# Another order of the filler matmuls of an attention stage, and its small constants loaded earlier

## The chip, the cores and the metric

The program runs on one core of a Trainium2 chip. The metric is the device time of one execution in microseconds (us). Three timed runs of the kernel before gave 2757.0, 2759.0 and 2761.09 us (median 2759.0); the profiled execution took 2755.99 us, with a span of 2753.8 us from the first to the last instruction.

## The reference

Two layers act on 1024 latent tokens and 256 context tokens of width 1024. Each layer normalises and modulates its input and multiplies it by one wide matrix; the columns of the product feed four branches, whose outputs are gated, projected, merged and added back.

```
z    = split_cols(h @ w_in)              # pool_in 256, mla_*, diff_*, swa_*, gates 1024, merge 4096
pool = windowed means (2, 4, 8, 16 tokens) of pool_in, minus pool_in, times w_pool, times s_pool
mla  = dense softmax attention over 1280 keys, 4 heads (latent branch)
diff = two dense softmax maps per head, map 1 - lam * map 2, 4 heads; normalised
       lam = exp(sum(lam_q1*lam_k1)) - exp(sum(lam_q2*lam_k2)) + lam_init
swa  = windowed attention, 128-token blocks, 256 context keys + up to 3 blocks, with a sink logit
x    = x + gate * rms_norm(sum_r sigmoid(merge_r) * ((y_r * silu(gates_r)) @ w_br[r]) @ w_out)
```

In layer 0 the 256 context tokens are queries too; in layer 1 only the 1024 latent tokens are.

## The kernel before, in words

Everything is fp32. A dense product is done as three matmuls per 128 rows of the contraction: a number is split into a rounded high part and the rest, and high*high, high*low and low*high are added (`mm3`, lines 75 to 78). TensorE (PE) does the matmuls, VectorE (DVE) maxima, differences and sums, ScalarE (ACT) exponentials, copies and the rounding, GpSimd (POOL) some elementwise work and the low parts of weights. Nearly all transfers are issued by one queue, SyncE's (SP). The instructions are emitted in the order in which the Python code runs; the framework then orders each engine's instructions by that order and by when it thinks their inputs ready, and puts in the semaphores. So code order sets the order on an engine, but an instruction that is ready earlier can be moved ahead.

A layer goes through these stages:

- the latent projections and their row statistics (`st.body` in `layer`);
- the dense part: a list of column tiles of `w_in`, built by `values`, `roped`, `keys_swa`, `gates` and `pooled`. Each tile is 128 columns times 8 contraction steps times 2 or 3 chunks of tokens (512, 512 and, where the context counts, 256). A step of 512 tokens is three matmuls and counts as 3 * 0.216 = 0.648 us in the planner's money. Tiles up to the queries of the differential branch (`dense.until(W_DQ + 1)`) are run at once, together with `up_all`, which makes the latent branch's keys, values and queries;
- the attention units: for each of the 4 heads of the differential branch, 4 of the latent branch and 2 key heads of the local (windowed) branch, one unit for each block of queries: 20, 20 and 20 units in layer 0, 16, 16 and 16 in layer 1. A unit has "mains" (scores of 128 queries, line 1116, 1075 to 1077 or 1174, and their softmax in `softmax`, line 977) and turns of `pv_steps` (transposes of the probabilities, line 1005, and their products with the values, line 1021), which run one to two units behind;
- merge of the branches, `w_out`, and the next layer's normalisation.

The dense tiles that are left when the units begin are filler. After each main and each turn the loop calls `dense.fill(f)`, which emits dense steps until their planned cost reaches f; f is `FILL[l][branch]` shared over the unit's mains and turns, so a unit with all its turns gets about `FILL[l][branch]` us of filler (keys 1, 2, 3: latent, differential, local branch). `FILL[l]["pre"]` is emitted ahead of the first unit. When the list is empty, nothing is filled. The keys of the local branch must be stored before its first unit is prefetched, so `prefetch` forces the list up to `W_SQ + 1` there.

`pooled` is two tiles of the matrix and, after each, `rest`, which forms the windowed sums of a chunk on DVE (6 operations per chunk in the first, 8 in the second), multiplies them by `w_pool` with three matmuls (tiles `pd<-sh,wph` and so on), and stores the result. It counts as 0.7 us per 512 tokens in the planner. Its input lies in a buffer (`zt1`) of which there is one, shared with `values` and `roped`.

Ahead of the first unit `prefetch(0)` issues the loads of the first keys (`kt`), values (`vt`) and queries (`qt`); then `const_loads` issues four loads of the lambda rows, one of the sinks and one of the mask of the local branch (`smask`); then the filler "pre", and then `const_values`, which computes lambda. The lambda rows lie in two of the five buffers `P` of the probabilities. The weights of each filler tile are loaded (`wraw`) by the same queue, rounded by ACT (`wh`), and their rests taken by POOL (`wl`).

Of the kernel before, what the change touches and what calls it, by code (L numbers as in the profile page):

```python
# [8 lines left out]
F = mybir.dt.float32  # L9
# [10 lines left out]
T = SEQ + CTX  # L20
# [12 lines left out]
def kernel(ctx: ExitStack, tc: tile.TileContext, A: dict, out: bass.AP):  # L33
# [467 lines left out]
    def layer(l, es_prev):  # L501
# [15 lines left out]
        def lat_tile(i, dt):  # L517
            return (p1 if i > 2 else p1b).tile([128, T], dt, name=f"n{i}", tag=f"n{i}")
# [247 lines left out]
        for j in range(7):  # L766
            gates(j)
        values(W_SV, svd, 0)
        keys_swa()
        roped(W_SQ, sqd, qch, 64 ** -0.5, 4, 32, ("C64", "S64"))  # L770
        pooled()
# [16 lines left out]

        gkv = gcol("g_ckv", 0, 128)
# [99 lines left out]
        def up_all():  # L889
            nonlocal kvh, kvl, q0h, q1h, q0l, q1l  # L890
            for us in key_rope():
                yield us
            kvh, kvl, q0h, q0l = (lat_tile(i, R) for i in (0, 3, 1, 4))
# [56 lines left out]
        ls = c1.tile([128, 2], F, name="ls")  # L950
        nlam = c1.tile([128, 1], F, name="nlam")
        sink = c1.tile([128, 4], F, name="sink")
        nsink = c1.tile([128, 4], F, name="nsink")
        lam = kp.tile([128, T], F, name="P", tag="P", bufs=5)[:, 0:128].rearrange("p (a c) -> p a c", a=4)
        lt = kp.tile([128, T], F, name="P", tag="P", bufs=5)[:, 0:64].rearrange("p (a c) -> p a c", a=2)

        def const_loads():
            for i, n in enumerate(("lam_q1", "lam_k1", "lam_q2", "lam_k2")):
                dma(lam[:, i], A[n][l:l + 1, :].broadcast_to([128, 32]))
            dma(sink, A["sink"][l:l + 1, :].broadcast_to([128, 4]))  # L960
            dma(smask, A["smask"])

        def const_values():
            lv = lam.rearrange("p (a b) c -> p a b c", b=2)
            tt(lt, lv[:, :, 0], lv[:, :, 1], ALU.mult)
            nc.vector.tensor_reduce(out=ls, in_=lt, axis=AX.X, op=ALU.add)
            act(ls, ls, AF.Exp)
            tt(nlam, ls[:, 1:2], ls[:, 0:1], ALU.subtract)
            ts(nlam, nlam, -lam_init, op0=ALU.add)
            ts(nsink, sink, -1.0)  # L970
# [249 lines left out]
        const_loads()  # L1220
# [3 lines left out]
        for i, (key, keys, load, run) in enumerate(units):  # L1224
# [3 lines left out]
            for a, main in enumerate(mains):  # L1228
                main()
                if a == 0:  # L1230
                    prefetch(i + 1)
                dense.fill(f)
# [284 lines left out]
        for q, (ci, d) in enumerate(steps):  # L1517
# [30 lines left out]
    FILL = ({1: 4.1, 2: 4.9, 3: 0.8, "n": 1.5, "uk": 1.2, "uq": 1.5, "uv": 2.0, "pre": 10.0},  # L1548
            {1: 4.3, 2: 4.9, 3: 0.8, "n": 2.5, "uk": 1.2, "uq": 1.5, "uv": 2.0, "pre": 8.0})
# [114 lines left out]
```

## Time and profile before

| what | value |
|---|---|
| median of 3 runs (lowest to highest) | 2759.0 us (2757.0 to 2761.09) |
| profiled execution, its time and its span | 2755.99 us, 2753.8 us |
| PE busy | 2618.1 us, 95% |
| DVE, ACT, POOL busy | 1517.9, 1184.7, 803.6 us |
| mean granted TensorE clock, share of full | 0.978 |
| moved by DMA | 322.27 MB, mean 117 GB/s |
| layer 0: differential, latent, local units begin (first score) | 248.6, 489.2, 709.7 us |
| layer 1: differential, latent, local units begin (first score) | 1699.6, 1911.7, 2121.2 us |

Busy time is the union of an engine's instructions. Matmuls are pipelined and their ends are modelled, so PE can be shown as busy and still not be at its peak; where two stretches do like work, their lengths say more than their busy time. "Idle before, releaser" is the time that an engine stood still ahead of an instruction and what the profile believes ended it.

### The profile page before, as it was taken

What the parts mean: (1) busy time and instruction counts of PE and PEld (TensorE: products, weight loads), DVE (VectorE), ACT (ScalarE), POOL (GpSimd) and SP (SyncE); (2) the same over time, 40 slices, a digit from 0 to 9 for tenths busy, and PEclk for the clock granted to TensorE, in tenths of its full rate; (3) what the DMA queues carried; (4) which work ended last, traced back from release to release, by engine and by line L of the source; (5) the groups of instructions that cost most, each with busy time, mean ns of one, the idle gap of its engine ahead of it and who ended that gap; (6) DMA issues with size and microseconds to landing.
All of it is one profiled execution on the core that took longest, in us unless ns stands there. A gap on an engine that the chain in (4) does not pass through costs nothing.

```text
span 2753.8 us, 38441 instructions
## 1 busy us (share of the span) xinstructions
PE 2618.1 (95%) x14194; PEld 2202.6 (80%) x14194; DVE 1517.9 (55%) x2638; ACT 1184.7 (43%) x2178; POOL 803.6 (29%) x492
## 2 busy tenths in 40 slices
PE   7998999999989989999999997999999999999998
PEld 5776888888878878888877776888877788888878
DVE  7545888766754893322148554888666732233133
ACT  4433777655662211222245343777555722222231
POOL 4223343110001223333324313443110022444324
PEclk9998999999999999999999998999999999999999
DMA  6366333532334552221135266333433243222123
GB/s 237 100 199 199 117 98 91 147 121 92 98 114 136 193 171 74 76 73 62 35 106 198 81 202 207 123 106 108 136 99 97 78 129 102 79 87 86 48 77 100
DMA packets 209069, 322.27 MB, mean 117 GB/s; under 512 B 26740, under 2 KB 123634, under 8 KB 208882
## 3 DMA queue, kind: packets, MB, share of 16 engines
q1 hardware_dynamic: 208882, 319.83, 37.1%
q8 instruction: 111, 1.82, 0.3%
q14 instruction: 76, 0.62, 0.1%
HBM read 239.07 MB, written 77.86 MB: 115 GB/s over the span
## 4 chain that ended last, share of the span: by engine, by line
PE 60%; DVE 10%; issue 4%; DMA 3%; ACT 3%; POOL 1%; SPq 0%; POOLq 0%; DVEq 0%; ACTq 0%
PE pd L76 12%; PE pd L77 12%; PE pd L78 11%; PE acc L1021 5%; PE pt L1005 4%; PE pt L76 2%; PE pt L77 2%; PE pt L78 2%; DVE mjunk L150 2%; PE pss L1116 1%; PE pss L1075 1%; PE pss L1077 1%; PE pss L1076 1%; PE pd L1532 1%; DVE t L53 1%
## 5 line engine op out<-in xcount | busy, mean ns | idle before, releaser
L76 PE MATMUL pd<-h,wh 128*128 128x512 f32 (+2 forms) x2288 | 859.0, 376 | 20.8 <-ACT zt L50 9.4
L77 PE MATMUL pd<-h,wh 128*128 128x512 f32 (+2 forms) x2288 | 846.0, 370 | 0.3 <-DVE h L56 0.3
L78 PE MATMUL pd<-h,wl 128*128 128x512 f32 (+2 forms) x2288 | 846.3, 370 | 0.0
L53 POOL TENSOR_TENSOR wl<-wraw,wh 128x1024 fp32r<-128x1024 f32 x106 | 260.5, 2457 | 995.6 <-ACT wh L50 929.3
L76 PEld LDWEIGHTS pd<-h,wh 128*128 128x128 f32 (+1 forms) x2288 | 437.1, 191 | 84.9 <-ACT zt L50 10.0
L78 PEld LDWEIGHTS pd<-h,wl 128*128 128x128 f32 (+1 forms) x2288 | 435.8, 190 | 67.3 <-issue 1.5
L77 PEld LDWEIGHTS pd<-h,wh 128*128 128x128 f32 (+1 forms) x2288 | 437.3, 191 | 59.2 <-DVE h L56 1.0
L977 DVE CUSTOM_DVE_ANT_0 P<-pss,zero 128x1280 f32<-128x1280 f32 (+1 forms) x216 | 295.9, 1370 | 98.3 <-PE pss L1116 45.7
L53 DVE TENSOR_TENSOR tl<-pt,th 128x512 fp32r<-128x512 f32 (+1 forms) x420 | 276.2, 671 | 132.5 <-ACT th L50 128.9
L50 ACT ACTIVATE th<-pt 128x512 fp32r<-128x512 f32 (+1 forms) x420 | 239.5, 582 | 159.1 <-PE pt L1005 153.7
L53 DVE TENSOR_TENSOR sg<-sg,pt 128x512 f32<-128x512 f32 x96 | 65.4, 686 | 394.8 <-PE pt L78 394.8
L1005 PE MATMUL pt<-kc,P 128*128 128x128 f32 x1632 | 255.8, 276 | 4.9 <-DVE P L56 1.2
L1021 PE MATMUL acc<-th,vt 128*128 128x256 f32 x816 | 244.8, 312 | 3.4 <-ACT ot L50 1.5
L1021 PE MATMUL acc<-tl,vt 128*128 128x256 f32 x816 | 221.6, 292 | 10.0 <-DVE tl L53 9.3
L50 ACT ACTIVATE wh<-wraw 128x1024 fp32r<-128x1024 f32 x124 | 130.7, 1054 | 214.4 <-PE pd L77 162.3
L50 ACT ACTIVATE P<-P,m 128x1280 f32<-128x1280 f32 (+1 forms) x144 | 182.8, 1269 | 76.7 <-DVE m L977 75.9
L50 ACT ACTIVATE sg<-pd 128x512 f32<-128x512 f32 x128 | 75.6, 591 | 316.2 <-PE pd L78 313.3
L1005 PEld LDWEIGHTS pt<-kc,P 128*128 128x128 f32 x1632 | 191.5, 141 | 20.4 <-DVE tl L53 6.1
L53 POOL TENSOR_TENSOR m<-m,sg 128x512 f32<-128x512 f32 x96 | 131.5, 1375 | 193.7 <-DVE sg L53 192.4
L1021 PEld LDWEIGHTS acc<-th,vt 128*128 128x128 f32 x816 | 155.5, 191 | 37.4 <-ACT th L50 20.5
L1021 PEld LDWEIGHTS acc<-tl,vt 128*128 128x128 f32 x816 | 155.7, 191 | 30.3 <-DVE tl L53 21.3
L50 ACT ACTIVATE P<-P,negm 128x1280 f32<-128x1280 f32 (+3 forms) x144 | 146.5, 1017 | 75.8 <-DVE negm L977 75.3
(291 smaller groups left out, 3917.8 us busy)
## 6 DMA issues: line engine op xcount, KB each, us to landing
wraw<-in_w_in_dram SPq DMA_DIRECT2D x108, 512.0 KB, 3.5
wmt<-in_w_modt_dram SPq DMA_DIRECT2D x64, 256.0 KB, 3.1
wraw<-in_w_out_dram SPq DMA_DIRECT2D x32, 512.0 KB, 3.3
yd<-ot SPq DMA_DIRECT2D x108, 128.0 KB, 1.8
kt<-dkd SPq DMA_DIRECT2D x64, 160.0 KB, 3.1
qt<-dqd SPq DMA_DIRECT2D x72, 128.0 KB, 2.8
ya<-yd SPq DMA_DIRECT2D x36, 256.0 KB, 3.0
yb<-yd SPq DMA_DIRECT2D x36, 256.0 KB, 3.0
```

Source lines behind the costliest of these rows:

```text
L50: return nc.scalar.activation(out=o, in_=i, func=func, **kw)
L53: return (e or nc.vector).tensor_tensor(out=o, in0=a, in1=b, op=op)
L76: nc.tensor.matmul(ps, wh(k), xh(k), start=k == 0, stop=False)
L77: nc.tensor.matmul(ps, wh(k), xl(k), start=False, stop=False)
L78: nc.tensor.matmul(ps, wl(k), xh(k), start=False, stop=k == n - 1)
L150: nc.vector.tensor_tensor_reduce(out=jk, in0=a, in1=b, scale=1.0, scalar=start, op0=ALU.mult, op1=ALU.add, accum_out=o)
L977: nc.vector.tensor_tensor_reduce(out=o, in0=i, in1=zero.to_broadcast([128, nk]) if mask is None else mask, scale=-1.0, scalar=1e30 if h is ...
L1005: t = nc.tensor.transpose(pt[:, 2 * j + i, :], Ps[i][:, (g + j) * 128:(g + j + 1) * 128], ident)
L1021: nc.tensor.matmul(acc, vt[:, kts[g + j], :], x[:, j, :], start=g + j == 0 and a == 0, stop=g + j == nk - 1 and a == 1)
L1075: nc.tensor.matmul(o, qt[0:96, 0, qs], kh[0:96, ks], start=True, stop=False)
L1076: nc.tensor.matmul(o, qt[0:96, 0, qs], kl[0:96, ks], start=False, stop=False)
L1077: nc.tensor.matmul(o, qt[0:96, 1, qs], kh[0:96, ks], start=False, stop=True)
```

## The change

- The tiles of the dense part get another order. Before: gates 0 to 6, values, keys and queries of the local branch, pooling, gate 7. After: gates 0 to 5, pooling, values, keys and queries of the local branch, gates 6 and 7.
- `FILL` is changed: local branch 0.8 to 1.4 in layer 0, 0.8 to 1.3 in layer 1; in layer 1 also the latent branch 4.3 to 3.7 and the differential branch 4.9 to 4.6.
- The four lambda rows and the sinks are loaded when the dense part is set up, into tiles of their own, and the two sums of lambda are taken in `up_all`; only the exponential and the last steps stay in `const_values`.
- The mask of the local branch is loaded at the third differential unit, once the fourth unit's inputs are requested.

```diff
--- before.py
+++ after.py
@@ -763,12 +763,13 @@
         values(W_DV + 1, dvd, 2)
         roped(W_DK, dkd, ALL, 1.0, 8, 16, ("C32", "S32"))
         roped(W_DQ, dqd.rearrange("m a d n -> a m d n"), qch, 32 ** -0.5, 8, 16, ("C32", "S32"))
-        for j in range(7):
+        for j in range(6):
             gates(j)
+        pooled()
         values(W_SV, svd, 0)
         keys_swa()
         roped(W_SQ, sqd, qch, 64 ** -0.5, 4, 32, ("C64", "S64"))
-        pooled()
+        gates(6)
         gates(7)
 
         p1b = pool(f"mlb{l}", 1, es_m)
@@ -786,6 +787,11 @@
             split(raw, h, lo)
             return h, lo
 
+        ls, nlam, sink, nsink = (sta.tile([128, w], F, name=n) for n, w in (("ls", 2), ("nlam", 1), ("sink", 4), ("nsink", 4)))
+        lam = p1.tile([128, 4, 32], F, name="lam")
+        for i, n in enumerate(("lam_q1", "lam_k1", "lam_q2", "lam_k2")):
+            dma(lam[:, i], A[n][l:l + 1, :].broadcast_to([128, 32]))
+        dma(sink, A["sink"][l:l + 1, :].broadcast_to([128, 4]))
         gkv = gcol("g_ckv", 0, 128)
         gq0 = gcol("g_cq", 0, 128)
         gq1 = gcol("g_cq", 128, 64)
@@ -890,6 +896,9 @@
             nonlocal kvh, kvl, q0h, q1h, q0l, q1l
             for us in key_rope():
                 yield us
+            lv = lam.rearrange("p (a b) c -> p a b c", b=2)
+            tt(lv[:, :, 0], lv[:, :, 0], lv[:, :, 1], ALU.mult)
+            nc.vector.tensor_reduce(out=ls, in_=lv[:, :, 0], axis=AX.X, op=ALU.add)
             kvh, kvl, q0h, q0l = (lat_tile(i, R) for i in (0, 3, 1, 4))
             q1h, q1l = (lat_tile(i, R)[0:64] for i in (2, 5))
             todo = [(0, c) for c in ALL] + [(1, c) for c in qch]
@@ -947,23 +956,8 @@
         c1 = pool(f"ac{l}", 1, es_a)
 
         smask = c1.tile([128, 768], F, name="smask")
-        ls = c1.tile([128, 2], F, name="ls")
-        nlam = c1.tile([128, 1], F, name="nlam")
-        sink = c1.tile([128, 4], F, name="sink")
-        nsink = c1.tile([128, 4], F, name="nsink")
-        lam = kp.tile([128, T], F, name="P", tag="P", bufs=5)[:, 0:128].rearrange("p (a c) -> p a c", a=4)
-        lt = kp.tile([128, T], F, name="P", tag="P", bufs=5)[:, 0:64].rearrange("p (a c) -> p a c", a=2)
-
-        def const_loads():
-            for i, n in enumerate(("lam_q1", "lam_k1", "lam_q2", "lam_k2")):
-                dma(lam[:, i], A[n][l:l + 1, :].broadcast_to([128, 32]))
-            dma(sink, A["sink"][l:l + 1, :].broadcast_to([128, 4]))
-            dma(smask, A["smask"])
 
         def const_values():
-            lv = lam.rearrange("p (a b) c -> p a b c", b=2)
-            tt(lt, lv[:, :, 0], lv[:, :, 1], ALU.mult)
-            nc.vector.tensor_reduce(out=ls, in_=lt, axis=AX.X, op=ALU.add)
             act(ls, ls, AF.Exp)
             tt(nlam, ls[:, 1:2], ls[:, 0:1], ALU.subtract)
             ts(nlam, nlam, -lam_init, op0=ALU.add)
@@ -1217,7 +1211,6 @@
 
         todo = []
         prefetch(0)
-        const_loads()
         dense.fill(FILL[l]["pre"])
         const_values()
         last.clear()
@@ -1229,6 +1222,8 @@
                 main()
                 if a == 0:
                     prefetch(i + 1)
+                    if i == 2:
+                        dma(smask, A["smask"])
                 dense.fill(f)
                 n = turns[a]
                 while todo and (todo[0][0] < i - 1 or a and n):
@@ -1545,8 +1540,8 @@
         es_l.close()
         return es_t
 
-    FILL = ({1: 4.1, 2: 4.9, 3: 0.8, "n": 1.5, "uk": 1.2, "uq": 1.5, "uv": 2.0, "pre": 10.0},
-            {1: 4.3, 2: 4.9, 3: 0.8, "n": 2.5, "uk": 1.2, "uq": 1.5, "uv": 2.0, "pre": 8.0})
+    FILL = ({1: 4.1, 2: 4.9, 3: 1.4, "n": 1.5, "uk": 1.2, "uq": 1.5, "uv": 2.0, "pre": 10.0},
+            {1: 3.7, 2: 4.6, 3: 1.3, "n": 2.5, "uk": 1.2, "uq": 1.5, "uv": 2.0, "pre": 8.0})
     TURNS = {1: (3, 2), 2: (2, 1, 1, 1), 3: (1, 2)}
     GY = (3.0, 1.5, 0.5)
     WMB = 6
```

## Rows read from the trace of the kernel before

**Rows 1.** The page, busy time of each engine: us, share of the span, instructions.

```profile
PE 2618.1 (95%) x14194; PEld 2202.6 (80%) x14194; DVE 1517.9 (55%) x2638; ACT 1184.7 (43%) x2178; POOL 803.6 (29%) x492
```

**Rows 2.** Who PE waited for, whole span: total us, times, longest us.

```profile
PE pss L1116 <- DMA P<-in_lam_k_dram: 7.2, 1, 7.2
PE pss L1116 <- DMA P<-in_lam_q_dram: 7.0, 1, 7.0
```

**Rows 3.** SP's queue at layer 0's first unit: start us, us, engine, transfer.

```profile
241.89 1.29 SPq L72 DMA_DIRECT2D qt<-dqd  x2
...
243.22 0.59 SPq L72 DMA_DIRECT2D P<-in_lam_q_dram  x1
...
245.28 0.43 SPq L72 DMA_DIRECT2D sink<-in_sink_dram  x1
...
247.66 0.33 SPq L72 DMA_DIRECT2D smask<-in_smask_dram  x1
...
248.03 0.43 SPq L72 DMA_DIRECT2D wraw<-in_w_in_dram  x1
```

**Rows 4.** Loads of qt, 220 to 260 us: time from issue to landing.

```profile
DMA to landing us min/median/max: 5.9/5.9/5.9
```

**Rows 5.** The other engines there, in order of time, idle before in brackets.

```profile
248.60 1.40 PE L1116 MATMUL pss<-kt,qt 128*128 128x512 f32 x3 [7.17 <-DMA P<-in_lam_k_dram]
...
251.60 1.43 PE L1116 MATMUL pss<-kt,qt 128*128 128x512 f32 x3 [1.59 <-DVE m L977]
...
253.53 1.06 ACT L50 ACTIVATE wh<-wraw 128x1024 fp32r<-128x1024 f32 x1 [0.49 <-DMA wraw<-in_w_in_dram]
...
254.66 2.38 POOL L53 TENSOR_TENSOR wl<-wraw,wh 128x1024 fp32r<-128x1024 f32 x1 [19.96 <-ACT wh L50]
```

**Rows 6.** Windows: length; busy PE, PEld, DVE, ACT, POOL (count); clock; DMA share; GB/s.

```profile
241.43:260.64 19.21, 8.12 (x19) 5.44 (x19) 5.45 (x13) 6.66 (x10) 4.64 (x3) 0.56 0.71 206
50.00:100.00 50.00, 46.15 (x235) 36.89 (x234) 34.69 (x69) 24.17 (x49) 19.11 (x16) 0.86 0.12 36
1500.00:1550.00 50.00, 43.13 (x235) 36.33 (x234) 37.01 (x66) 22.50 (x45) 15.21 (x15) 0.93 0.40 124
```

**Rows 7.** Windows: three local units of layer 0, three of layer 1.

```profile
732.91:746.55 13.64, 13.64 (x95) 12.12 (x93) 9.77 (x21) 9.88 (x25) 0.00 (x0) 1.00 0.22 64
2144.20:2156.34 12.14, 11.71 (x87) 10.06 (x86) 10.37 (x21) 10.08 (x25) 0.00 (x0) 1.00 0.22 65
```

**Rows 8.** Windows of the dense matmuls alone (tile pd).

```profile
732.91:746.55 13.64, 4.33 (x13) 2.23 (x13) 0.00 (x0) 0.00 (x0) 1.00 0.22 64
2121.20:2197.57 76.37, 0.28 (x1) 0.09 (x1) 0.27 (x1) 0.00 (x0) 1.00 0.35 97
1684.00:1692.00 8.00, 8.00 (x37) 6.61 (x36) 0.00 (x0) 0.58 (x1) 1.00 0.76 222
```

**Rows 9.** Windows: a latent unit without pooling, then the stretches with it.

```profile
627.45:640.38 12.93, 12.93 (x81) 11.38 (x79) 5.86 (x9) 6.41 (x13) 0.00 (x0) 1.00 0.09 27
649.37:661.65 12.28, 10.16 (x62) 8.32 (x61) 11.93 (x18) 7.96 (x14) 2.74 (x1) 1.00 0.52 152
696.78:709.73 12.95, 9.56 (x57) 8.31 (x56) 11.39 (x21) 8.15 (x19) 4.08 (x1) 0.87 0.56 161
2035.08:2047.65 12.57, 10.19 (x63) 8.30 (x62) 12.38 (x20) 7.87 (x15) 2.69 (x1) 1.00 0.52 154
2075.40:2098.14 22.74, 17.83 (x86) 14.91 (x84) 17.74 (x26) 11.02 (x19) 1.77 (x1) 0.85 0.22 72
```

**Rows 10.** Windows: a unit at the end of the differential branch, layer 0.

```profile
470.41:482.99 12.58, 12.20 (x73) 9.97 (x72) 11.56 (x19) 9.13 (x17) 6.57 (x4) 1.00 0.24 73
```

**Rows 11.** Timeline of DVE and POOL in layer 1's second pooling.

```profile
2074.78 2.40 POOL L53 TENSOR_TENSOR wl<-wraw,wh 128x1024 fp32r<-128x1024 f32 x1 [25.27 <-PE pt L1005]
...
2075.28 3.07 DVE L53 TENSOR_TENSOR t<-up 128x527 f32<-128x527 f32 x2 [0.61 <-ACT up L50]
...
2078.28 0.69 DVE L53 TENSOR_TENSOR t<-t 128x525 f32<-128x525 f32 x1
```

## The prediction, made before the changed kernel was run

> **What bounds the kernel now.** I read the page first: PE is busy for 2618.1 us, 95% of the 2753.8 us span [rows 1]. Since the change neither adds nor removes a matmul, all that it can win or lose lies in the 135.7 us in which PE is idle, and in the stretches in which the clock is low or the matmuls wait for each other behind a busy bar. Then I read PE's waits for the whole span. Two of the longest single waits, 7.2 and 7.0 us, stand ahead of the first scores of layer 0 and of layer 1 and carry the name of the lambda rows [rows 2], which the change moves. The scores don't read these rows, so I looked at SP's queue: qt is issued from 241.89 us, the lambda rows only behind it, from 243.22 us, and behind them the sinks, the mask and the next filler weights wraw at 248.03 us [rows 3]. A qt load there needs 5.9 us to land [rows 4]. The second is issued near 242.5 us, so it lands near 248.4 us, and the scores start at 248.60 us [rows 5]: it is qt that ends this wait, and qt is not changed. The windows by stage came last; they stand below with the part that they price.
>
> **1. The first unit (lambda rows, sinks, mask).** Six requests leave the queue between qt and wraw. What starts earlier is not the first score but the filler behind it. In layer 0 ACT waits 0.49 us for wraw and starts to round it at 253.53 us, POOL makes the low part until 257.04 us (254.66 + 2.38), and meanwhile PE stands idle 1.59 us ahead of the second score group [rows 5]; the third and fourth group wait likewise. Over 241.43 to 260.64 us PE is busy for 8.12 of 19.21 us, and the granted clock is 0.56 of full, a mix of 1.2 and 2.4 GHz, while the windows inside the branch show 1.00 [rows 6, 10]. Wraw could be issued at 243.2 us in place of 248.03 us, but its 512 KB queue behind the data of vt and qt: at the 206 GB/s of this window they need 2.5 us after 248.4 us, so it lands near 251.0 us instead of near 253.5 us. Bounds for one layer: 0.5 us if ACT keeps its order (it waited 0.49 us only), 4.8 us if the whole shift of the issue arrives, with some low clock besides. I take 2.3 us, just under the 2.5 us of the landing, to which it is nearest. Layer 1 has the same order and the same gap [rows 2], so twice: **minus 4.6 us** (minus 1 to minus 9.6).
> The loads themselves go to the start of the dense part: five requests of 0.43 to 0.59 us of SP [rows 3], 2.5 us in each layer. What is queued behind them there are weights and norm rows. The DMA share around the place is 0.12 in layer 0 and 0.40 in layer 1 [rows 6], so I cost them at nothing; without that cover they cost up to 2.5 us twice. The two DVE operations on lambda leave the first unit for the latent work (0.4 us, hidden, or 0.4 us lost). The mask goes behind the fourth unit's inputs and is read only in the local branch, over 400 us later: nothing.
>
> **2. The filler of the local branch in layer 1.** The planner's sums decide where the filler falls. A step of 512 tokens counts 0.648 us. In layer 1 a gate is 16 steps or 10.4 us; 8 gates (83.0), local values and keys (25.9), local queries (20.7) and pooling (20.7 + 2.8) are 153.1 us. Before: 8.4 are spent ahead of the units, 16 units of 4.9 take 78.4, and 16 of 4.3 could take 68.8 but find 66.3. The list is empty before the local branch, and the trace agrees: one dense matmul in 2121.20 to 2197.57 us [rows 8]. After: 8.4 + 16 x 4.6 + 16 x 3.7 = 141.2, rounded up by whole steps to 141.4; 11.7 us, 18 steps or 54 matmuls, are left for the local branch. A dense matmul takes 0.22 us where PE does nothing else (37 in 8.00 us [rows 8]), so 11.9 us of PE leave stretches in which PE is full.
> What do they cost in the local branch? Three inner units of layer 0 with 13 filler matmuls (2.9 us) last 13.64 us; three of layer 1 with none last 12.14 us [rows 7, 8]. So 2.9 us of filler lengthen them by 1.5 us, and 48% is hidden. 48% of 11.9 us: **minus 5.7 us**. Bounds: 0 if the matmuls are moved ahead of their place into the end of the latent branch, minus 11.9 us if the branch hides all.
>
> **3. Layer 0's FILL.** Differential and latent branch keep 4.9 and 4.1, so the same 11.0 us are left for the local branch, only spent in about 8 units instead of 15. DVE work and scores don't change. Units that get more hide a little more, units that get none a little less: 0, within 2 us to either side.
>
> **4. Pooling, from the end of the latent branch to the end of the differential branch.** This is the part that can go wrong. `rest` counts 0.7 us in the planner but is a burst on DVE: one pooling operation takes 0.69 us [rows 11], and 6 operations per chunk (one of them a half copy, taken as 0.4 us) are 3.9 us, 8 are 5.2 us. With 2.5 chunks in layer 0 and 2 in layer 1 that makes 9.7 + 13.1 and 7.7 + 10.5 us of DVE. Before, these bursts fall into the latent branch, where a clean unit of 12.93 us has DVE busy for 5.86 us and PE for all of it; the four stretches with pooling leave PE idle for 2.1, 3.4, 2.4 and 4.9 us, and the clock falls to 0.87 and 0.85 in two of them [rows 9]. Together 12.8 us, and at most 5.1 us more for the clock (12.95 x 0.13 + 22.74 x 0.15): 13 to 18 us that leave this place.
> After, by the same sums of the planner, the first burst falls on units 17 and 18 of 20 in layer 0 and 13 and 14 of 16 in layer 1, and the second on the first latent units. At the end of the differential branch DVE is busy for 11.56 of 12.58 us [rows 10]: 1.0 us of room, 2 in two units. What doesn't fit is 7.7 and 5.7 us. The second burst has 7 us of room in a latent unit, leaving 6.1 and 3.5 us. That is 23 us. Against it, the local values and keys leave just these units: in the first burst's place their differences, some 3 us of DVE in each layer (an estimate: 10 pieces of half the 0.69 us), go. About 17 us, against 13 to 18 before: I take **plus 2 us**. Bounds: minus 6 us, if PE takes filler ahead as it waits, and plus 20 us (rival below).
> The page SBUF of the Trainium skill, section "Practical consequences", speaks against this part: DVE with two SBUF inputs and GpSimd reading SBUF take one port in turn, each for a whole instruction. The trace agrees: two pooling sums that begin during a POOL operation end after it and take 3.07 us together, against 0.69 us for one alone [rows 11].
>
> **The sum.** -4.6 - 5.7 + 0 + 2 = -8.3 us on the profiled execution's 2756.0 us (span 2753.8 and 2.2 around it): 2747.7 us. The median of the runs shown is 3.0 us higher, so 2750.7, say **2751 us**.
>
> **Rivals.**
> A, slower: pooling makes DVE the bound where the differential branch ends. The point from which it decides is DVE's room: 1.0 us in 12.58, while POOL is busy for 6.57 of the same 12.58 us [rows 10], and a pooling sum that meets POOL loses about 1.7 us (3.07 less twice 0.69 [rows 11]). If each layer loses two such meetings (7 us in all) and all four bursts stay exposed but for the 6 us of room (41 + 7 - 6 = 42), 42 stand against 22 before (18 and the neighbours that also ran short): +20 on this part, -10.3 on the others, so about +10: 2769 us. For it: differential units are full on both PE and DVE. Against: PE has filler to take while it waits.
> B, no difference: ACT keeps the exponential ahead of the rounding in the first unit (-1 instead of -4.6), and the port costs pooling 7 us more than I take (+9 instead of +2). -1 - 5.7 + 9 = +2: 2761 us. For it: in the profile the exponential does stand ahead and wraw is only 0.49 us late.
> C, the named wait is real: the lambda loads slow qt after all, and 7.2 + 7.0 us go. -14.2 - 5.7 + 2 = -18: 2741 us. Against it: they are issued behind qt.
> D, the layer 1 filler doesn't reach the local branch, moved ahead by the framework: -4.6 + 2 = -2.6: 2756 us.
>
> **Chances.** Forecast 0.50, A 0.14, B 0.18, C 0.08, D 0.10. A difference under 0.2%, 5.5 us, can't be told from none: faster means below 2753.5 us, slower above 2764.5 us. The forecast's own range is 2744 to 2756; four fifths of it (0.40), all of C and a few hundredths of D and of errors in B's terms give faster 0.53. B and D otherwise, and the rest of the forecast, give same 0.32, A and a little of B slower 0.15. The range that leaves out half of C and two thirds of A is 2741 to 2765 us.
>
> **What would show it.** Part 1: wraw issued within 2 us of qt in the first unit, its rounding ahead of 252 us by the old clock, the wait ahead of the first score still about 7 us, now under another name. If that wait falls to 2 us, C holds. Part 2: some 54 dense matmuls in layer 1's local branch, which lasts about 6 us longer than 76.4 us, while its differential and latent branches together get about 12 us shorter. Part 4: the pooling matmuls stand before the latent branch's first units; the latent units at its old place have no idle PE, and PE's idle time around the new place sums to some 17 us. The prediction is wrong if layer 0 between its first score and its merge gets longer by more than 5 us, or if the first units' gaps don't change.

## The result, and the profile after

The changed kernel takes 2800.91 us (median of four runs, 2799.57 to 2804.92); the kernel before took 2759.77 us beside it (four runs, 2757.0 to 2761.09). The ratio is 1.0152, 95% interval 1.0139 to 1.0165: 41 us slower, where 2751 us was forecast and 2765 us was the top of the range. The profiled execution of after has a span of 2800.4 us against 2753.8 us, so the trace has 46.6 us to place.

The page of after, busy time of each engine, answers to [rows 1]:

```profile
PE 2636.1 (94%) x14194; PEld 2218.1 (79%) x14194; DVE 1538.3 (55%) x2638; ACT 1187.5 (42%) x2178; POOL 799.1 (29%) x492
```

Neither PE's nor DVE's count has changed, yet DVE is busy for 20.4 us more: some of its instructions last longer. The span by stages, from first score to first score, is what placed the loss:

| from first score to first score (local: to the branch's last products), us | before | after |
|---|---|---|
| layer 0: differential, latent, local | 240.6, 220.6, 98.3 | 253.1, 232.7, 100.1 |
| layer 1: differential, latent, local | 212.1, 209.5, 76.4 | 226.4, 209.2, 80.6 |

The start is 2.0 us later (first score at 250.58 us for 248.60 us), layer 0's units take 26.4 us more and layer 1's 18.2 us more. Inside the differential branches the first fifteen (layer 0) and twelve (layer 1) units are as before to within 3 us in all; the last five and four, where pooling now falls, take 68.1 us for 52.8 and 67.3 us for 50.1. The windows of those stretches in after (columns as in [rows 6]; in layer 0 most of the units 16 to 18, in layer 1 the last four without their end) stand against the 12.58 us unit of [rows 10], in which PE was busy for 12.20 us at full clock:

```profile
437.50:478.90 41.40, 29.19 (x127) 21.40 (x126) 39.19 (x61) 25.93 (x42) 16.36 (x7) 0.75 0.29 90
1886.96:1936.00 49.04, 34.53 (x158) 27.92 (x157) 41.71 (x59) 26.68 (x42) 16.35 (x8) 0.79 0.25 76
```

In layer 0 DVE is busy for 39.19 of 41.40 us: it has become the bound there. In layer 1 it is 41.71 of 49.04 us. In layer 0 PE issues 127 matmuls in 41.40 us, 3.1 per us, where [rows 10] has 73 in 12.58, 5.8 per us. It stands idle for 12.2 us there and 14.5 us in layer 1, and the mean granted clock of the stretches is 0.75 and 0.79 of full, a mix of 1.2 and 2.4 GHz. The same stretches for the dense matmuls alone (tile pd) in after:

```profile
437.50:478.90 41.40, 3.92 (x8) 1.46 (x7) 0.00 (x0) 1.74 (x3) 0.75 0.29 90
1886.96:1936.00 49.04, 10.14 (x26) 5.84 (x26) 0.00 (x0) 1.96 (x3) 0.79 0.25 76
```

Of the eight in 41.40 us six are pooling's own products, and two are the last of the first pooling tile: no other filler comes out. What doesn't come out here comes later. The dense matmuls of layer 0's differential and latent branch, before and then after:

```profile
248.60:489.20 240.60, 135.65 (x542) 87.93 (x542) 0.00 (x0) 11.86 (x23) 0.97 0.36 112
489.20:709.79 220.59, 86.07 (x335) 52.23 (x335) 0.00 (x0) 9.72 (x18) 0.98 0.39 119
```

```profile
250.58:503.69 253.11, 125.13 (x486) 79.44 (x486) 0.00 (x0) 12.14 (x23) 0.94 0.33 104
503.69:736.40 232.71, 103.21 (x407) 63.94 (x406) 0.00 (x0) 10.63 (x20) 0.98 0.37 113
```

So the differential branch is longer with 56 of them fewer, and the latent branch has 72 more, 15.8 us at 0.22 us each [rows 8], and is 12.1 us longer.

Who PE waited for, whole span (total us, times, longest us), first before, then after:

```profile
PE pss L1116 <- DVE m L977: 7.1, 5, 1.6
```

```profile
PE pss L1110 <- DVE m L971: 23.4, 16, 6.3
PE pss L1110 <- DMA qt<-dqd: 12.8, 2, 6.9
PE pd L76 <- ACT sh L50: 5.6, 5, 3.7
```

Scores (line 1116, now 1110) that wait for DVE's maxima went from 5 waits to 16. How one such round runs is in the timeline of after, PE, DVE and POOL, the second unit with pooling (start, length, idle before in brackets):

```profile
446.06 0.79 PE L76 MATMUL pd<-sh,wph 128*128 128x512 f32 x1 [0.57 <-ACT sh L50]
446.27 2.90 POOL L53 TENSOR_TENSOR P<-P 128x1280 f32<-128x1280 f32 x1
...
447.02 2.70 DVE L53 TENSOR_TENSOR sl<-tab,sh 128x512 fp32r<-128x512 f32 x1
447.08 1.44 PE L1110 MATMUL pss<-kt,qt 128*128 128x512 f32 x3 [0.23 <-DVE m L971]
449.64 0.68 DVE L53 TENSOR_TENSOR tab<-t,tab 128x512 f32<-128x512 f32 x1
449.77 0.80 PE L77 MATMUL pd<-sl,wph 128*128 128x512 f32 x1 [1.26 <-DVE sl L53]
450.25 1.48 DVE L971 CUSTOM_DVE_ANT_0 P<-pss,zero 128x1280 f32<-128x1280 f32 x1
450.37 0.63 PE L78 MATMUL pd<-sh,wpl 128*128 128x512 f32 x1
```

The scores end at 448.52 us, but their maximum starts only at 450.25 us, since DVE has the low part `sl` (2.70 us, beside a POOL operation until 449.17 us) and a division (0.68 us) ahead of it. The next scores wait for that maximum until 451.79 us. From score group to score group it is 4.71 us, where the unit of [rows 10] takes 12.58 us for four, 3.15 each. PE's product with `sl` stands between two score groups, too, and waits 1.26 us for DVE, but the scores behind it wait longer, for their maximum. The Trainium skill, page "PSUM — Partial Sum Buffer", section "Engine vs sequencer instructions", says that matmuls start in program order, so that nothing behind a waiting product passes it; the trace agrees, no matmul starts in those 1.26 us.

That the low part is stretched by POOL is seen in the DVE operations of pooling (minimum, median, maximum ns), before and then after:

```profile
L53 DVE TENSOR_TENSOR tab<-t,tab x10: 409/675/692, 648.5 to 2088.1; 128x512 f32<-128x512 f32 x8, 128x256 f32<-128x256 f32 x2
L53 DVE TENSOR_TENSOR sl<-tab,sh x10: 422/685/692, 654.4 to 2093.9; 128x512 fp32r<-128x512 f32 x8, 128x256 fp32r<-128x256 f32 x2
```

```profile
L53 DVE TENSOR_TENSOR tab<-t,tab x10: 421/680/3151, 440.7 to 1970.5; 128x512 f32<-128x512 f32 x8, 128x256 f32<-128x256 f32 x2
L53 DVE TENSOR_TENSOR sl<-tab,sh x10: 419/680/2701, 447.0 to 1974.7; 128x512 fp32r<-128x512 f32 x8, 128x256 fp32r<-128x256 f32 x2
```

Summed over all 70 of pooling's DVE operations (60 for sums, copy, division and subtraction, 10 low parts) that is 56.1 us in after and 47.8 us in before. So 8.3 of DVE's 20.4 us more lie in pooling itself, the rest elsewhere.

### The profile page after: what moved, and what is told of

It reads as the page before. It is cut to its first block, busy times and chain, and to the rows that moved or that the text cites. A ratio compares the mean times of both kernels' runs of the same rounds, so it can differ in the third digit from the quotient of the medians.

```text
span 2800.4 us, 38452 instructions
## 1 busy us (share of the span) xinstructions
PE 2636.1 (94%) x14194; PEld 2218.1 (79%) x14194; DVE 1538.3 (55%) x2638; ACT 1187.5 (42%) x2178; POOL 799.1 (29%) x492
## 5 line engine op out<-in xcount | busy, mean ns | idle before, releaser
L76 PEld LDWEIGHTS pd<-h,wh 128*128 128x128 f32 (+1 forms) x2288 | 438.4, 192 | 88.2 <-ACT zt L50 10.6
L1015 PEld LDWEIGHTS acc<-tl,vt 128*128 128x128 f32 x816 | 157.1, 192 | 29.6 <-DVE tl L53 19.5
```

The source lines that it names most:

```text
L76: nc.tensor.matmul(ps, wh(k), xh(k), start=k == 0, stop=False)
L1015: nc.tensor.matmul(acc, vt[:, kts[g + j], :], x[:, j, :], start=g + j == 0 and a == 0, stop=g + j == nk - 1 and a == 1)
```

## The experiments

Each ratio is to the kernel before on the same chip, with its 95% interval. "Order", "constants" and "FILL" are the three parts of the diff.

### The parts, one at a time

**e1_order_only.** The kernel before with the new order alone.

```diff
-        for j in range(7):
+        for j in range(6):
             gates(j)
+        pooled()
...
-        pooled()
+        gates(6)
         gates(7)
```

> The kernel before with the new order of the tiles alone (gates 0 to 5, pooling, local values, keys and queries, gates 6 and 7); FILL and the constants as before. Theory S (the pooling's chain on VectorE falls where the differential branch keeps VectorE full, and as the filler is one serial list nothing else is to be had for TensorE meanwhile): 40 us or more over before, 2800 us or more. Rival F (the new FILL is what costs): within 8 us of before. Rival K (the early constants cost): within 8 us of before.

2803.2 us, 1.0163 (1.0146 to 1.0180), 43 us more than before, as theory S had it: the order alone is the whole loss.

**e2_const_only.** The early lambda rows and sinks and the late mask alone, as in the diff; order and FILL of before.

> The changed kernel with the old order and the old FILL: only the early lambda rows and sinks and the late mask are left of the change. S: 3 to 6 us under before, from the first units (2753 to 2757 us). K: 10 us or more over before.

2755.73 us, 0.9983 (0.9974 to 0.9992): 4.8 us less than the 2760.52 us of before beside it. Part 1 of the prediction, minus 4.6. In its trace the differential branches, where the first units lie, last 237.1 and 210.0 us in place of 240.6 and 212.1.

**e3_fill_only.** The new FILL alone.

```diff
-    FILL = ({1: 4.1, 2: 4.9, 3: 0.8, ...
-            {1: 4.3, 2: 4.9, 3: 0.8, ...
+    FILL = ({1: 4.1, 2: 4.9, 3: 1.4, ...
+            {1: 3.7, 2: 4.6, 3: 1.3, ...
```

> The kernel before with the new FILL alone. S and the prediction: some 6 us under before (54 matmuls of layer 1 move into its local branch, half of them hidden; 2750 to 2757 us), nothing in layer 0. F: 20 us or more over before.

2764.33 us, 1.0015 (1.0005 to 1.0024): 4 us more, where parts 2 and 3 had -5.7 together. -4.8 + 3.8 + 42.7 = 41.7 for the three parts alone, 41.1 measured together: they add.

**e4_pool_late.** After, with pooling alone put back behind the local queries.

```diff
             gates(j)
-        pooled()
         values(W_SV, svd, 0)
...
+        pooled()
         gates(6)
```

> The changed kernel with pooling put back behind the local queries (gates 0 to 5, local values, keys, queries, pooling, gates 6 and 7); new FILL and early constants kept. S: the loss goes whole and the two small gains stay, 2745 to 2755 us. F or K: still 2785 us or more.

2762.04 us, 1.0006 (0.9995 to 1.0017): above the 2755 us that was the most expected, but 38.9 us under after. Pooling's place is nearly all of the order; the two gates at the end are not. Its layer 0 differential branch takes 247.0 us against 237.1 us in e2, now that local values and keys fall there.

### What of pooling is dear: the list, or DVE's time

**e6_rest_beside.** In after, pooling's sums and products are no longer a link of the filler list but come out beside the matmuls of the gates, a little after each step; two of the six gates follow pooling's tiles, so that there are such matmuls.

```diff
                     act(keep[j][:, pos(c0):pos(c0) + n], ps)
+                    if (c0, n) == qch[-1]:
+                        vals.add(rests[j](), 2.0)
...
-                dense.add(f"pool{j}", None, rest)
+                rests[j] = rest
```

> The changed kernel with pooling still inside the differential branch, but its window sums no longer a link of the filler list: they are emitted piece by piece beside a gate's matmuls (gates 0 to 3, first pooling tile, gate 4, second pooling tile, gate 5, then as changed). The work is the same. Theory S1 (the serial list starves TensorE: nothing else can be filled until the sums are through): half or more of the 41 us comes back, 2780 us or less. Theory S2 (the sums' time on a full VectorE is the loss, whoever waits for it): 2795 us or more, since VectorE has the same work in the same branch.

2799.05 us, 1.0139 (1.0124 to 1.0154): nothing gained, as theory S2 had it. But the run changes more than the list. Pooling's second tile, which in after falls into the latent branch, now falls into the differential branch as well (265.3 us in layer 0, after 253.1), and pooling's DVE operations sum to 68.0 us (after 56.1). Beside the first tile the gates' matmuls do come out, and the clock stays at full:

```profile
369.00:413.00 44.00, 38.35 (x215) 30.53 (x214) 42.69 (x68) 29.61 (x50) 18.54 (x8) 1.00 0.34 102
```

The six units around it take 79.0 us (359.11 to 438.08 us), where the same six took 74.1 us in before without pooling (362.33 to 436.40). The last five, with the second tile, take 76.2 us for 52.8. So the run doesn't show what the list alone costs.

**e8_sums_pool.** In after, the sums, the division and the subtraction run on GpSimd (the copy stays on DVE).

```diff
-                        tt(a[:, 1:w], up[:, 0:w - 1], up[:, 1:w], ALU.add)
+                        tt(a[:, 1:w], up[:, 0:w - 1], up[:, 1:w], ALU.add, nc.gpsimd)
```

> The changed kernel with the window sums, the division and the subtraction on GpSimd in place of VectorE (the copy and the split stay). S2: VectorE is relieved of most of pooling, 2770 to 2785 us. S1: the chain gets longer (a GpSimd sum of this size takes 1.3 to 1.8 us against 0.7), so the filler is cut off as long or longer, 2795 us or more.

2789.52 us, 1.0109 (1.0090 to 1.0127): 11 us less than after, between the ranges of the two theories. DVE's busy time falls by 24.4 us and POOL's grows by 56.2 us, as the page of this kernel shows:

```profile
PE 2627.5 (94%) x14194; PEld 2211.2 (79%) x14194; DVE 1513.9 (54%) x2588; ACT 1184.3 (42%) x2178; POOL 855.3 (31%) x542
```

The chain got longer on the slower engine while DVE got room; the run changes both and so settles neither.

**e9_sums_twice_new** and **e10_sums_twice_old.** The sums, the copy and the division done twice, in after and in before.

```diff
-                        tt(a[:, 1:w], up[:, 0:w - 1], up[:, 1:w], ALU.add)
+                        for _ in range(2):
+                            tt(a[:, 1:w], up[:, 0:w - 1], up[:, 1:w], ALU.add)
```

> The changed kernel with pooling's window sums, copy and division done twice, with the same values: some 28 us more of VectorE (4 and 6 operations per chunk once more, 2.5 and 3.9 us per 512 tokens), all of it in the place that the change gave to pooling. S2 (VectorE is the bound there): 25 to 45 us over the changed kernel, 2825 to 2845 us. If VectorE has room there and the loss is of another kind: under 12 us more.

> The kernel before with the same sums done twice: the same 28 us of VectorE at the end of the latent branch. S2, with the room that a latent unit leaves on VectorE: 5 to 20 us over before, clearly less than in the new place. If a VectorE operation costs the same wherever it stands: as much as in the new place.

e9: 2832.7 us, 1.0257 (1.0242 to 1.0272), 32 us over after. e10: 2787.51 us, 1.0095 (1.0082 to 1.0108), 27 us over before, a miss: I had expected the old place to hide most of it. The pages of e9 and then of e10 show DVE busy for 34.8 and 30.6 us more than in after and before:

```profile
PE 2645.8 (93%) x14194; PEld 2227.1 (79%) x14194; DVE 1573.1 (56%) x2688; ACT 1187.9 (42%) x2178; POOL 798.5 (28%) x492
```

```profile
PE 2630.4 (94%) x14194; PEld 2210.3 (79%) x14194; DVE 1548.5 (56%) x2688; ACT 1184.6 (43%) x2178; POOL 800.0 (29%) x492
```

In both places a further microsecond of pooling on DVE costs about 0.9 us of time (32/34.8, 27/30.6). What differs is therefore not the price of more, but of the first set; with it DVE is already busy for 11.93 of 12.28 us in the old place [rows 9]. The next runs take it away.

### Pooling taken apart

**e7_rest_bare** (after), **e13_bare_old** (before), **e14_bare_new_order** (e1) and **e15_bare_late** (e4). Sums, copy, division and subtraction go, and with them the load of the counts that the division takes (in after's stretch, 437 to 485 us, none of DVE's waits is for a load); the raw values are split.

```diff
-                        tt(a[:, 1:w], up[:, 0:w - 1], up[:, 1:w], ALU.add)
...
-                        tt(t1, t1, up[:, 8:8 + n], ALU.subtract)
...
-                        spl(t1, lambda h: hl_...
+                        spl(up[:, 8:8 + n], lambda h: hl_...
```

> The changed kernel with the window sums, the division and the subtraction left out of pooling (its input goes straight into the split and the matmuls), so the output is not the reference's: 1 VectorE operation per chunk in place of 6 and 8, the matmuls and their place unchanged. S1 and S2: the loss goes, 2765 us or less. A loss that lies in the matmuls' place or in FILL: still 2785 us or more.

> The kernel before with pooling's window sums, division and subtraction left out (as in the run with the changed kernel, so the output is not the reference's): what these VectorE operations cost in the old place. Theory R (the old place has a fixed room for a first burst, the new one none): 2742 to 2750 us, 10 to 18 us under before, so that the move exposes some 25 us more of the same sums. Theory E (they cost the same wherever they stand, as the doubled sums suggest): 2725 us or less, and the loss of the move is not theirs.

> The kernel before with the new order alone and the same operations left out: against the run with the old order and none of them, what the new order costs without the sums. Theory R: 2755 to 2762 us, 40 us or more under the new order with the sums; the order without the sums costs up to 12 us more than the old. Theory E: the order costs 35 us or more without the sums too.

> The change with pooling back behind the local queries, and with pooling's sums, division and subtraction left out (the raw values are split instead, so the output differs). The same kernel with the sums took 2762.0 us, and the change without the sums 2756.8. Theory H (half of the loss is other pooling work than the sums, that also runs worse in the early place): the sums cost here what they cost in the old kernel, 23.5 us, so 2738.5 us, some 18 below the change without sums. Rival G (the place costs only through the sums): 2752 to 2757, as fast as the change without sums.

e7: 2756.81 us, 0.9987 (0.9977 to 0.9996). e13: 2737.3 us, 0.9917 (0.9900 to 0.9933). e14: 2758.48 us, 0.9991 (0.9982 to 1.0001). e15: 2743.7 us, 0.9935 (0.9918 to 0.9952). So the sums cost 44.7 us in the new place (2803.2 - 2758.48; 44.1 by after and e7), but 24.0 us in the old one (2761.33 of before beside it, less 2737.3) and 18.3 us in e4's (2762.04 - 2743.7). e13 and e15 fall between the ranges of their theories. Without the sums the new order still costs 21 us (e14 less e13), where theory R allowed 12, and the new place is 13 us behind the late one (e7 less e15): the sums are half to two thirds of the loss, not all.

**e16_no_products_new** (e7) and **e17_no_products_late** (e15). The split into high and low part and pooling's products go as well (30 of them, six of 256 columns, so as much as 27 of 512: 6 us).

```diff
-                        spl(up[:, 8:8 + n], lambda h: hl_...
-                        ps = dense_ps(n)
-                        mm3(ps, lambda k: wph[:, j], ...
...
-                        act(yv, ps, scale=spc[:, j:j + 1])
+                        act(yv, up[:, 8:8 + n], scale=spc[:, j:j + 1])
```

> The change without pooling's sums, and without the split into high and low part and the 27 pooling matmuls (the raw values are scaled and stored, so the output differs). PE loses about 6 us of matmuls (27 at 0.22). Theory P (the chain from ACT over VectorE to PE in the early place holds the filler): more than those 6 us go, 2756.8 falls to about 2738. Rival U (the single buffer of the pooled values and the shifted neighbours): 2749 to 2752, the 6 us and no more.

> The same without sums, split and pooling matmuls, but with pooling behind the local queries. Theory P: the chain costs little here beside its 6 us of matmuls, so about 2732, and the early place is then 6 us or less behind. Rival U: about 2732 as well, with the early place still 15 to 20 us behind.

e16: 2730.22 us, 0.9887 (0.9873 to 0.9902). e17: 2736.64 us, 0.9905 (0.9890 to 0.9920). In the new place split and products cost 26.6 us (e7 less e16), four times their matmuls; in the late place 7.1 us (e15 less e17), about their matmuls. Without either the early place is level with the late one or a little better, though pooling's tiles and their single buffer are still there: rival U is out. The 38.9 us of pooling's place are taken apart by this:

| pooling's work, us | new place | late place | difference |
|---|---|---|---|
| sums, copy, division, subtraction | 44.1 | 18.3 | 25.8 |
| split and products | 26.6 | 7.1 | 19.5 |
| the tiles themselves, and what moves with them | (2730.2) | (2736.6) | -6.4 |

Each difference comes from four medians whose ratios are known to 0.1 to 0.2%, 3 to 5 us, so the split is good to some 7 us. In e16's trace the units 16 to 18 take 34.57 us (in after 43.3, from 435.55 to 478.89), with PE full and the clock at full, and filler fills the gaps. The stretch in e16, then for its dense matmuls alone:

```profile
430.70:465.27 34.57, 34.33 (x210) 29.10 (x209) 29.07 (x48) 27.14 (x44) 15.80 (x8) 1.00 0.38 117
```

```profile
430.70:465.27 34.57, 20.02 (x89) 13.78 (x87) 0.00 (x0) 1.56 (x3) 1.00 0.38 117
```

**e18_pool_after_gates.** After, with all eight gates ahead of pooling, so that pooling falls into the first half of the latent branch, still ahead of the local operands.

```diff
-        for j in range(6):
+        for j in range(8):
             gates(j)
         pooled()
...
-        gates(6)
-        gates(7)
```

> The change with all eight gates ahead of pooling, so that pooling falls into the first half of the latent branch, still ahead of the local values, keys and queries. Theory D (the full differential units are what makes the place dear): 2758 to 2768, near the 2762.0 of pooling behind the queries. Rival O (any place ahead of the local operands is dear, for the tiles they share): 2785 or more.

2766.01 us, 1.0014 (1.0003 to 1.0024): 35 us under after, near the late place. What is dear is the end of the differential branch with the units right behind it (e18 moves both bursts), not a place ahead of the local operands. Its layer 0 differential branch takes 237.1 us (after 253.1), and pooling's low part is nowhere stretched (all 70 operations sum to 47.8 us, as in before); the row of e18 stands against the one of after above:

```profile
L53 DVE TENSOR_TENSOR sl<-tab,sh x10: 419/680/693, 512.8 to 1994.2; 128x512 fp32r<-128x512 f32 x8, 128x256 fp32r<-128x256 f32 x2
```

### A better version

**e5_gates_first.** The constants of e2, and the list: eight gates, local values, keys, queries, pooling (`gates(7)` moved up); FILL of before.

> For a better version: early constants, old FILL, and all eight gates ahead of local values, keys, queries and pooling, so that in the differential branch, where VectorE is full, the filler is nothing but matmuls. S1 and S2: 3 to 10 us under the version with the early constants alone, 2745 to 2752 us. If only pooling matters and the local values don't: the same as that version, 2754 to 2757 us, or worse where pooling now runs into the local branch.

2752.71 us, 0.9972 (0.9961 to 0.9982): 3.0 us under e2, which the intervals do not tell from none.

**e11_fill_layer1.** e2 with the new FILL for layer 1 alone.

> The early constants with the new FILL of layer 1 alone (3.7, 4.6, 1.3), old order, old FILL in layer 0. The prediction's part 2: 5.7 us under the version with the early constants, near 2750 us. If the differential branch does not get shorter by the filler that leaves it: within 2 us of that version, or above it; then the loss of the new FILL alone lies in layer 1. If it gains, the loss lies in layer 0.

2753.29 us, 0.9973 (0.9965 to 0.9982), 2.4 us under e2, which the intervals do not tell from none. Against e3 it has the old FILL in layer 0, and 11 us less time; 4.8 of them are the constants, which e3 lacks. The rest, 6 us (known to some 4), is what 1.4 costs in layer 0.

**e12_best.** e2; in layer 0 the list of e5 and the old FILL, in layer 1 the old list and a FILL between the two.

```diff
-        for j in range(7):
+        for j in range(7 + (l == 0)):
             gates(j)
...
-        gates(7)
+        if l:
+            gates(7)
...
-            {1: 4.3, 2: 4.9, 3: 0.8, ...
+            {1: 3.6, 2: 4.9, 3: 1.3, ...
```

> For a better version: early constants; layer 0 with all eight gates ahead of local values, keys, queries and pooling and the old FILL; layer 1 in the old order with the differential branch at 4.9 as before, the latent branch at 3.6 and the local branch at 1.3. If the differential branch's filler should be matmuls and the local branch of layer 1 can hide filler: 2744 to 2750 us, under both kernels. If only the constants help: 2753 to 2757 us.

2748.61 us (six runs), 0.9958 (0.9942 to 0.9974): faster than both kernels, 12 us under before and 52 us under after. Its margin over e5 and e11 lies inside the intervals.

## Why the prediction was wrong

**What bounds the kernel now: right.** The wait ahead of the first score was qt's, not that of the lambda rows. With these gone it is still there, under the name that it should have had. After, first unit of layer 0 (first score, and ACT's rounding of the filler's weights):

```profile
250.58 1.40 PE L1110 MATMUL pss<-kt,qt 128*128 128x512 f32 x3 [5.90 <-DMA qt<-dqd]
...
252.83 1.06 ACT L50 ACTIVATE wh<-wraw 128x1024 fp32r<-128x1024 f32 x1 [10.32 <-DMA wraw<-in_w_in_dram]
```

7.17 us became 5.90 us: rival C, which wanted this wait gone, is out. So is rival B's first half, by part 1.

**Part 1, right (-4.6 forecast, -4.8 in e2).** That the two agree to 0.2 us is luck, as e2's interval runs from -2.2 to -7.2. SP's queue in after shows wraw 0.05 us behind the first qt, as the prediction asked (within 2 us), against 4.9 us in [rows 3]:

```profile
245.09 1.30 SPq L72 DMA_DIRECT2D qt<-dqd  x2
246.44 0.59 SPq L72 DMA_DIRECT2D wraw<-in_w_in_dram  x1
```

By the first score, the rounding starts 2.25 us after it in place of 4.93 us: 2.7 us earlier in one layer, where 2.3 us was taken. The gap after it closes in part: the window of after that answers to the first one of [rows 6] has PE busy for 11.19 us in place of 8.12, at 0.73 of the clock in place of 0.56.

```profile
243.40:262.60 19.20, 11.19 (x44) 8.44 (x43) 5.90 (x8) 6.37 (x9) 4.69 (x2) 0.73 0.81 248
```

**Part 2, right on where the filler goes and what it costs there; the gain is not shown.** In after the local branch of layer 1 has the matmuls that the planner's sums gave (56 for 54), against one in [rows 8]:

```profile
2163.37:2243.97 80.60, 17.68 (x56) 8.96 (x54) 0.27 (x1) 1.76 (x3) 1.00 0.35 101
```

So rival D is out. It lasts 4.2 us longer than before, where 6.2 was forecast. In e11, with pooling at its old place, it lasts 14.9 us longer than in e2 (90.9 for 76.0), but 10.6 of them lie in the branch's first two units, in e11 and then in e2:

```profile
2109.01:2134.23 25.22, 19.69 (x114) 16.72 (x112) 19.77 (x35) 13.52 (x27) 2.94 (x1) 0.86 0.39 113
2115.62:2130.21 14.59, 12.91 (x93) 11.11 (x92) 9.96 (x20) 9.41 (x20) 0.00 (x0) 1.00 0.60 171
```

There it is not filler that lengthens them: with less spent earlier, pooling's second burst is what is left of the old list, and falls into these units (DVE is busy for 19.77 us in place of 9.96). The rest of the branch has 39 more matmuls, 8.6 us at 0.22, and lasts 4.3 us longer: half is hidden, close to the 48% of the prediction. Differential and latent branch get 15 us shorter (406.1 for 421.1). The gain of e11, -2.4 us, can't be told from none; -5.7 was forecast. What was left out is that in the old order the smaller FILL pushes pooling, too, and not only matmuls; what it is worth in the new order no run shows.

**Part 3, wrong (0 within 2 forecast, about +6 by e3 and e11).** The sentence that failed is that units that get more hide more and units that get none a little less. In e3 the filler of layer 0's local branch is spent in its first eight units, and the second key head starts without any; the stretch of its first four units in e3, then e2's:

```profile
758.36:784.73 26.37, 17.40 (x83) 14.37 (x81) 10.81 (x25) 14.69 (x32) 0.00 (x0) 0.74 0.42 120
```

```profile
752.56:777.01 24.45, 18.49 (x111) 15.02 (x110) 11.22 (x24) 17.11 (x36) 2.37 (x1) 0.94 0.50 145
```

28 matmuls fewer take 1.9 us more, at a granted clock of 0.74 in place of 0.94. The branch as a whole takes 104.7 us against 98.3 us. e11, with the old FILL there, also shows 13.6 us of low clock in this branch and 99.6 us, so the clock alone doesn't explain the 6 us; the rest of it stays open.

**Part 4, the step that failed: "I take plus 2 us", with +20 as the upper bound, where the order costs +43.** The place was right (the first burst falls from the 16th of 20 units and the 13th of 16 on, forecast 17th and 13th), and so was the bound that DVE becomes, which rival A named. Three terms of the sum were off, and a fourth was left out.

- The exposed time was "what doesn't fit", 23 us, as if the rest were free: a unit's room of 1.0 us in 12.58 us was set against the burst. In the new place the sums alone cost 44.7 us, nearly all of the 46.8 us that they take on DVE in e1's trace; in the old place 24.0 of 41.5 us, in e4's 18.3 of 40.1. The burst itself was put at 41 us with the low parts, where before's trace has 47.8. Scores that wait for a maximum wait for what DVE does ahead of it. PE's clock falls besides (31.2 us at 1.2 GHz in layer 0's differential branch, 12.0 before); which part of the loss is the clock's, no run separates.
- The split and the products were not priced at all, being the same in number. In the new place they cost 26.6 us, in the late place 7.1 us (e16, e17). Their matmuls are 6 us, their low parts 9.2 us on DVE (e7). That the rest comes from products that wait in PE's queue between score groups is argued, not shown; they also share the two `pd` buffers with the filler, which no run tests.
- The relief was taken at 13 to 18 us, the idle time and the clock of the four stretches of [rows 9]. But the local values, keys and queries fall into these units now and leave PE idle in their turn. Four of the units of after around the old place, the ones with the most idle time:

```profile
661.56:674.70 13.14, 11.19 (x65) 9.86 (x64) 10.15 (x16) 5.69 (x14) 2.99 (x2) 0.87 0.49 156
687.62:702.39 14.77, 11.28 (x47) 9.52 (x47) 8.53 (x11) 6.94 (x12) 4.17 (x3) 0.77 0.39 111
2107.93:2122.36 14.43, 12.76 (x78) 10.92 (x77) 10.86 (x15) 7.81 (x15) 3.04 (x2) 1.00 0.58 173
2122.36:2137.20 14.84, 11.84 (x74) 10.18 (x72) 10.39 (x12) 7.05 (x14) 5.33 (x3) 1.00 0.19 63
```

  PE stands idle for 10.1 us in them (1.95 + 3.49 + 1.67 + 3.00), with a clock of 0.87 and 0.77 in two. It was 12.8 us and 0.87 and 0.85 before: little relief.
- The port was left out of the sum; only the rivals priced it, at 7 us. Pooling's own DVE operations got 8.3 us longer, so the price was about right. (All of DVE got 20.4 us longer, but e4, with pooling late, is already 12.4 us over before.) The Trainium skill, page "SBUF — State Buffer", section "Who interferes with whom", on whose practical consequences the prediction drew, has a DVE instruction with two SBUF inputs contend with a GpSimd instruction that reads SBUF. The trace agrees: the low part of 0.68 us lasts 2.70 us and ends 0.55 us after the POOL operation that it met. In e18, in the latent branch, no low part lasts over 693 ns. The row that the prediction read for it was half misread: of the two sums of 3.07 us in [rows 11] only the first met the POOL operation and took 2.46 us; the second began after it and took 0.70. The row of before with the shortest and the longest of the two (ns):

```profile
L53 DVE TENSOR_TENSOR t<-up x2: 696/1576/2455, 2075.3 to 2077.7; 128x527 f32<-128x527 f32 x2
```

"PE has filler to take while it waits", my argument against rival A, did not come true: beside pooling's own products no filler came out for 41.40 us. Why the emitted order leaves PE without filler there was not isolated. In e6 PE has filler beside the first tile, and those units get 4.9 us longer with some 13 us of pooling on DVE; so filler at hand may well lower the price, but the run's second tile keeps its total from showing it. Layer 0's units got 26.4 us longer, where more than 5 was to show the prediction wrong. Of the checks that the prediction named, "PE idle some 17 us around the new place" read 26.7 us, and the latent units at the old place, which were to have no idle PE, have 10.1 us. Rival A had the mechanism and its place; its price of +20 on this part was less than half of what was measured.

## What to carry to other kernels

Price a moved burst by the chain that it joins, not by the idle share of its engine: in units whose scores wait for DVE, DVE operations ahead of a maximum can cost nearly their full length (44.7 us for 46.8 here), and a few small products several times their own (26.6 us for 6). Before a move, take the burst out in both places, sums and products apart; such runs gave 44 us in one place for 18 in the other, and 27 for 7. A place vacated is only worth what the next thing put there leaves free.

## Not expected

- Even in the latent branch, where DVE was busy for 5.86 of 12.93 us in a clean unit [rows 9], doubled pooling costs 27 us for 30.6 us of DVE (e10); the first set had taken the room.
- Moving the sums to GpSimd saves 11 us in the dear place although POOL gets 56.2 us more work (e8).
